# Issuing the later adaLN weight rows from ScalarE's queue instead of the sync engine's

## The chip, the cores and the metric

The kernel runs on one core of one Trainium2 chip, one launch, float32 inputs and output. The metric is the device time of one execution in microseconds (us). The kernel before was timed three times: 1854.41, 1858.54 and 1861.12 us, so the median is 1858.54 us. One execution was profiled; it took 1855.95 us, of which 1854.2 us lie between its first and its last instruction (the span).

## The reference, cut to what matters

One transformer-like layer on 256 tokens of width 2048: a SwiGLU feed-forward (inner width 5632), a token mixer (8 heads of attention with forget gates beside 4 heads of a chunked mLSTM), and a second feed-forward. Each of the three is preceded by a layer norm that is modulated, and followed by a gated residual sum and another layer norm. The modulation comes from one vector `c`, through a matrix of 2048 x 18432 ("ada"):

```python
ada = (jax.nn.silu(c) @ w_ada + b_ada)[:, None, :]
sh1, sc1, g1, sh2, sc2, g2, sh3, sc3, g3 = jnp.split(ada, N_ADA, axis=-1)
h = _swiglu(_modulate(x, sh1, sc1), ffn1_w_in, ffn1_w_out)
x = _layernorm(ALPHA * x + 0.5 * (1 + g1) * h, ln1_g, ln1_b)
h = _token_mixer(_modulate(x, sh2, sc2), w_in, ...)
x = _layernorm(ALPHA * x + (1 + g2) * h, ln2_g, ln2_b)
h = _swiglu(_modulate(x, sh3, sc3), ffn2_w_in, ffn2_w_out)
x = _layernorm(ALPHA * x + 0.5 * (1 + g3) * h, ln3_g, ln3_b)
```

The nine parts of `ada` (three shifts, three scales, three gates) are each 2048 wide. Which of them is needed when is what matters here: `sh1, sc1` before the first feed-forward, `g1` and `sh2, sc2` at its end, `g2` and `sh3, sc3` at the end of the mixer, `g3` at the very end.

## The kernel before, in words

**Weights.** Every weight matrix is streamed through SBUF once, in tiles of 1 MB called `raw` (three buffers, lines 402 to 430). ScalarE rounds half a tile to a `hi` part (the cast at line 155), VectorE subtracts to get the `lo` part (line 156), and TensorE makes three products of each (`hi*hi`, `hi*lo`, `lo*hi`, lines 443 to 447), which keeps float32 accuracy. `hi` and `lo` tiles are 128 x 1024, with six buffers each. A `raw` tile of the first feed-forward gives 24 matmuls of 512 columns: 4 blocks of rows, 2 halves of the tokens, 3 products. A buffer of `raw` is free once both of its `lo` parts are made; a buffer of `hi` is free once TensorE has used it.

**Ada rows.** The matrix `w_ada` is not multiplied on TensorE. It is cut into 18 units of 1024 columns, and each unit into 16 rows of blocks, 128 x 1024 elements or 512 KB. Each such row is loaded into one of two `araw` buffers, and VectorE adds `row * silu(c)` into an accumulator (lines 166 to 171). A unit ends with a split of the accumulator (`ahi`, `alo`, through the same line 155 on ScalarE), a sum over the partitions on TensorE (line 183) and a few VectorE operations. The first four units (the first shift and scale) are loaded at the start by other code. The other 14, 224 rows, are "the later ada rows": they go through `ask` (lines 188 to 192), which takes the next row of the list, gives it an `araw` buffer and issues its load. `ada_rows` (lines 194 to 200) accumulates row k and then asks for row k + 1, whose buffer is that of row k - 1. So the load of a row waits until VectorE has finished the row two before it.

**Pace.** The rows are woven in between the steps over weights: after each 1 MB step, `pump(rate)` lets `rate` rows through on average (line 815: `R_F, R_IN, R_OUT, R_MX, R_A, R_B = 1.25, 1.27, 1.12, 1.26, 1, .7`). `ada.stage` counts the boundaries that were passed: it is 0 during the first feed-forward, set to 1 (line 1198) after the boundary between it and the mixer, and set to 2 (line 1678) after the boundary between the mixer's output projection and the second feed-forward. A boundary is the stretch of residual sum, layer norms and modulation in which TensorE has little to do.

**What sets the order.** Each engine runs its instructions in its own order, and an instruction that has to wait holds up all that stand behind it on that engine. The issue of a DMA is an instruction too, of the engine whose queue it is given to: `SP.dma_start` goes to SyncE, which does nothing else, `S.dma_start` to ScalarE, `G_.dma_start` to GpSimd. A planner orders the instructions of each engine from dependencies and from costs that it assumes, except inside `tc.manual_schedule(...)` blocks, where the written order holds for the named engines (VectorE and ScalarE in the boundaries, lines 685 to 734), and except for `tc.issue_after(...)`, which only puts an instruction behind another on the same engine. The rows are paced with `pinned()` (lines 146 to 151): it ties to instructions of VectorE, so it orders the accumulations and not the loads. Before the change SyncE's queue holds, in one order, the loads of all weights and of the later ada rows. ScalarE issues no DMA at all; beside the casts it does the activations, copies out of PSUM and the copies of transposed tiles.

Of the kernel before, what the change touches and what calls it, by code (L numbers as in the profile page):

```python
# [14 lines left out]
P = 128  # L15
# [17 lines left out]
def layer_kernel(  # L33
# [8 lines left out]
    V, S, G_, PE, SP = nc.vector, nc.scalar, nc.gpsimd, nc.tensor, nc.sync  # L42
# [143 lines left out]
    wanted, asked = [], []  # L186

    def ask():
        if wanted:
            shape, src, tag, k = wanted.pop(0)  # L190
            asked.append(ap.tile(shape, F32, tag="araw", bufs=2, name=f"ar{tag}_{k}"))
            SP.dma_start(asked[-1], src[k * P:(k + 1) * P])

    def ada_rows(acc):
        for k in range(KD):
            if not asked:
                ask()
            ada_acc(acc, asked.pop(0), k)
            ask()
            yield  # L200
# [101 lines left out]
    ada = AdaQueue()  # L302
# [1511 lines left out]
```

## Time and profile before

| | |
|---|---|
| median of the three timed runs | 1858.54 us |
| the profiled execution's own time / its span | 1855.95 us / 1854.2 us |
| TensorE (PE) busy | 1820.5 us, 98% of the span |
| VectorE (DVE) busy | 1452.9 us, 78% |
| ScalarE (ACT) busy | 926.3 us, 50% |
| GpSimd (POOL) busy | 61.7 us, 3% |
| moved by DMA | 510.44 MB, 275 GB/s on average |
| issues of later ada rows on SyncE (line 192) | 224, from 220.6 to 1499.1 us |
| of these before the first boundary / between the two / after the second | 99 / 71 / 54 |

How to read it: busy is the union of an engine's instructions. The records of matmuls overlap, since they are pipelined; a stop of TensorE is seen in the rows that give the idle time before an instruction and what ended it. "SPq" in a row is SyncE's queue; it counts as never busy, and its waits are listed apart. A row "A <- B" in a list of waits means that A stood idle until B had ended; the numbers are the sum in us, how often, and the longest. In rows of the timeline: start, duration (both us), engine, line, operation, what it writes `<-` what it reads, how many were merged, and in brackets the idle time of the engine just before and what ended it.

### The profile page before, as it was taken

The page shows a single profiled execution, that of the slowest core. Times are in us where ns is not written, and L with a number is a line of the kernel's source. Part 1 is how long each engine was busy: PE and PEld are TensorE (multiplying, and loading weights), DVE is VectorE, ACT ScalarE, POOL GpSimd, SP SyncE. Part 2 cuts the span into 40 slices and gives each one's busy share as a digit, 9 for nine tenths or more (in the row PEclk, how much of TensorE's full clock was granted, in tenths as well). Part 3 has the DMA queues.
Part 4 walks back from the last instruction along what each step waited for, and adds up shares of the span by engine and source line. Part 5 has one row for each costly group of instructions (what it writes and reads, how often), then busy time and mean ns, then how long its engine had stood idle before and what let it go on. Part 6 is the DMA issues. An engine that isn't in the chain of part 4 may idle for free.

```text
span 1854.2 us, 25052 instructions
## 1 busy us (share of the span) xinstructions
PE 1820.5 (98%) x9577; PEld 1599.3 (86%) x9577; DVE 1452.9 (78%) x1787; ACT 926.3 (50%) x1332; POOL 61.7 (3%) x92
## 2 busy tenths in 40 slices
PE   7999999999999999999999999999999999999997
PEld 4888888888888888699999887888889999988887
DVE  6889989877787787788889888787997766564655
ACT  3554455443554344755666645555465444554441
POOL 1211100000000000000000000000000000000000
PEclk9999999999999999999999999999999999999999
DMA  9989978988988898489979883998877876666663
GB/s 364 379 293 328 328 231 304 328 308 299 312 294 276 304 305 315 151 295 320 325 264 307 327 298 117 326 347 287 303 255 254 274 233 201 205 204 201 203 202 144
DMA packets 242927, 510.44 MB, mean 275 GB/s; under 512 B 10834, under 2 KB 52466, under 8 KB 241784
## 3 DMA queue, kind: packets, MB, share of 16 engines
q1 hardware_dynamic: 234696, 477.90, 74.7%
q0 software_dynamic: 8112, 30.95, 4.8%
q8 instruction: 75, 1.23, 0.3%
q14 instruction: 44, 0.36, 0.0%
HBM read 506.71 MB, written 2.10 MB: 274 GB/s over the span
## 4 chain that ended last, share of the span: by engine, by line
PE 56%; DVE 1%; issue 1%; ACT 0%; DMA 0%; POOL 0%; DVEq 0%; ACTq 0%; POOLq 0%; SPq 0%
PE gu_f L450 8%; PE o_f L446 4%; PE o_f L445 4%; PE o_f L447 4%; PE gu_f L451 4%; PE fh L446 4%; PE fh L447 4%; PE fh L445 4%; PE o_mx L445 1%; PE o_mx L446 1%; PE o_mx L447 1%; PE b_mv L445 1%; PE b_fv L445 1%; PE pr_m L445 1%; PE b_mv L446 1%; PE b_fv L446 1%
## 5 line engine op out<-in xcount | busy, mean ns | idle before, releaser
L170 DVE SCALAR_TENSOR_TENSOR acc<-ar,csil,acc 128x1024 f32<-128x1024 f32 (+1 forms) x167 | 211.7, 1269 | 65.8 <-DMA ar<-in_w_ada_dram 65.4
L450 PE MATMUL gu_f<-x_f,hi_f2i 128*128 128x512 f32 x640 | 210.0, 382 | 0.0
L451 PE MATMUL gu_f<-x_f,lo_f2i 128*128 128x256 f32 x640 | 174.5, 273 | 0.0
L156 DVE TENSOR_TENSOR lo_f2o<-raw_f2o,hi_f2o 128x1024 fp32r<-128x1024 f32 x86 | 105.2, 1224 | 86.7 <-ACT hi_f2o L155 86.6
L155 ACT CAST hi_s<-raw_s 128x1024 fp32r<-128x1024 f32 x96 | 99.1, 1047 | 117.4 <-PE s L447 64.8
L155 ACT CAST hi_f1o<-raw_f1o 128x1024 fp32r<-128x1024 f32 x86 | 88.4, 1047 | 120.6 <-PE o_f L447 63.3
L155 ACT CAST hi_f2o<-raw_f2o 128x1024 fp32r<-128x1024 f32 x86 | 90.1, 1047 | 115.6 <-PE o_f L447 107.0
L446 PE MATMUL s<-lo_s,x_f 128*128 128x512 f32 x384 | 146.2, 381 | 1.2 <-DVE lo_s L156 1.1
L445 PE MATMUL s<-hi_s,x_f 128*128 128x512 f32 x384 | 146.4, 383 | 0.2 <-ACT x_f L359 0.2
L447 PE MATMUL s<-hi_s,x_f 128*128 128x512 f32 x384 | 145.5, 379 | 0.0
L156 DVE TENSOR_TENSOR lo_f2i<-raw_f2i,hi_f2i 128x1024 fp32r<-128x1024 f32 x80 | 97.9, 1224 | 54.2 <-ACT hi_f2i L155 53.7
L450 PEld LDWEIGHTS gu_f<-x_f,hi_f2i 128*128 128x128 f32 x640 | 121.0, 189 | 16.8
L445 PE MATMUL o_f<-hi_f1o,hi 128*128 128x512 f32 x344 | 131.4, 382 | 3.1 <-DVE hT L1021 2.0
L447 PE MATMUL o_f<-hi_f1o,lo 128*128 128x512 f32 x344 | 131.0, 381 | 0.0
L446 PE MATMUL o_f<-lo_f1o,hi 128*128 128x512 f32 x344 | 131.0, 381 | 0.0
L155 ACT CAST hi_f1i<-raw_f1i 128x1024 fp32r<-128x1024 f32 x80 | 81.1, 1045 | 99.4 <-DMA raw_f1i<-in_ffn_w_in_dram 71.8
L170 DVE SCALAR_TENSOR_TENSOR gate<-ar,csil,gate 128x1024 f32<-128x1024 f32 (+1 forms) x94 | 117.5, 1251 | 16.3 <-DMA ar<-in_w_ada_dram 15.9
L156 DVE TENSOR_TENSOR lo_s<-raw_s,hi_s 128x1024 fp32r<-128x1024 f32 x96 | 115.9, 1220 | 14.8 <-ACT hi_s L155 14.8
L445 PE MATMUL o_f<-hi_f2o,hi 128*128 128x512 f32 x332 | 125.8, 379 | 0.0
L446 PE MATMUL o_f<-lo_f2o,hi 128*128 128x512 f32 x332 | 125.8, 379 | 0.0
L447 PE MATMUL o_f<-hi_f2o,lo 128*128 128x512 f32 x332 | 125.8, 379 | 0.0
L155 ACT CAST hi_fh<-raw_fh 128x1024 fp32r<-128x1024 f32 x80 | 82.4, 1048 | 81.3 <-DMA raw_fh<-in_ffn_w_in_dram 37.0
(447 smaller groups left out, 4830.7 us busy)
## 6 DMA issues: line engine op xcount, KB each, us to landing
ar<-in_w_ada_dram SPq DMA_DIRECT2D x230, 512.0 KB, 5.5
raw_s<-in_ffn_w_in_dram SPq DMA_DIRECT2D x47, 1024.0 KB, 7.6
raw_f1o<-in_ffn_w_out_dram SPq DMA_DIRECT2D x44, 1024.0 KB, 7.3
raw_f2o<-in_ffn_w_out_dram SPq DMA_DIRECT2D x44, 1024.0 KB, 5.0
raw_f1i<-in_ffn_w_in_dram SPq DMA_DIRECT2D x40, 1024.0 KB, 7.5
raw_fh<-in_ffn_w_in_dram SPq DMA_DIRECT2D x40, 1024.0 KB, 7.4
raw_f2i<-in_ffn_w_in_dram SPq DMA_DIRECT2D x40, 1024.0 KB, 5.8
ar<-in_w_ada_dram POOLq DMA_DIRECT2D x45, 512.0 KB, 6.3
```

The costliest lines, as they stand in the source:

```text
L155: S.copy(hi, src)
L156: return V.tensor_tensor(out=lo, in0=src, in1=hi.bitcast(F32), op=ALU.subtract)
L170: V.scalar_tensor_tensor(out=acc, in0=raw, scalar=csil[:, k:k + 1], in1=acc, op0=ALU.mult, op1=ALU.add)
L445: PE.matmul(o, ah, bh, start=start, stop=False)
L446: PE.matmul(o, ah, bl, start=False, stop=False)
L447: PE.matmul(o, al, bh, start=False, stop=stop)
L450: PE.matmul(o, ah, x.rearrange("p s (a n) -> p s n a", a=2), start=start, stop=False)
L451: PE.matmul(o[:, T:], al, woven(x[:, 0]), start=False, stop=stop)
```

## The change

One line: where `ask` issues the load of a row, the queue is chosen by the stage. In stage 1 (the mixer and its output projection) it stays SyncE's; before the first boundary and after the second it is ScalarE's.

```diff
     def ask():
         if wanted:
             shape, src, tag, k = wanted.pop(0)
             asked.append(ap.tile(shape, F32, tag="araw", bufs=2, name=f"ar{tag}_{k}"))
-            SP.dma_start(asked[-1], src[k * P:(k + 1) * P])
+            (SP if ada.stage == 1 else S).dma_start(asked[-1], src[k * P:(k + 1) * P])
```

Nothing else is edited: the rows, their buffers, their pace and the accumulations are the same. The planner orders the whole program anew.

## The prediction

> **What bounds the kernel now.** I read first the page's span and engine rows (busy us, share of the span, instructions), then the busy times by stage.
>
> ```profile
> span 1854.2 us, 25052 instructions
> PE 1820.5 (98%) x9577; PEld 1599.3 (86%) x9577; DVE 1452.9 (78%) x1787; ACT 926.3 (50%) x1332; POOL 61.7 (3%) x92
> ```
>
> The stages are the first feed-forward with its later rows (215 to 750), the first boundary, the mixer (790 to 1128), the second boundary, the second feed-forward with rows, and the rest. After the stretch: TensorE, its weight loads, VectorE, ScalarE, GpSimd busy, then granted clock, DMA share, GB/s.
>
> ```profile
> 215.00:750.00 535.00, 529.83 (x2499) 462.11 (x2498) 431.97 (x450) 242.14 (x302) 6.31 (x10) 1.00 0.86 299
> 750.00:790.00 40.00, 37.39 (x151) 24.43 (x150) 33.37 (x78) 34.78 (x73) 3.06 (x4) 1.00 0.36 123
> ...
> 1160.00:1510.00 350.00, 350.00 (x1809) 311.38 (x1808) 283.03 (x316) 188.91 (x267) 2.20 (x4) 1.00 0.85 290
> 1510.00:1855.00 345.00, 333.78 (x1747) 298.03 (x1746) 208.16 (x235) 147.20 (x174) 4.11 (x4) 0.99 0.58 193
> ```
>
> TensorE sets the end: the change can win only where TensorE stands idle in the two row stretches, and that is 535 - 529.83 = 5.2 us in the first and nothing in the second. TensorE's waits in the first stretch name it all:
>
> ```profile
> PE o_f L445 <- DVE hT L1021: 2.0, 1, 2.0
> PE gu_f L446 <- DVE lo_f1i L156: 1.2, 2, 0.7
> PE o_f L445 <- DVE res L556: 1.1, 1, 1.1
> PE cp L854 <- DVE acc L170: 0.4, 1, 0.4
> PE bc L183 <- DVE alo L156: 0.4, 1, 0.4
> ```
>
> The longest of these cost more than its own length, as the clock granted just after it shows:
>
> ```profile
> 523.55 0.48 PE L445 MATMUL o_f<-hi_f1o,hi 128*128 128x512 f32 x1 [1.97 <-DVE hT L1021]
> ```
> ```profile
> 525.00:530.00 5.00, 5.00 (x17) 4.06 (x16) 4.72 (x5) 3.40 (x6) 0.00 (x0) 0.68 0.65 212
> ```
>
> After 1.97 us of idleness the clock stood at 0.68 for 5 us, 0.32 x 5 = 1.6 us more. So all that can be won is 5.1 + 1.6 = 6.7 us.
>
> **What is moved.** The issues of line 192 on SyncE, first stretch and then second:
>
> ```profile
> L192 SPq DMA_DIRECT2D ar<-in_w_ada_dram x99: 327/367/500, 220.6 to 734.1; - x99
> ...
> DMA to landing us min/median/max: 3.7/5.4/8.8
> ```
> ```profile
> L192 SPq DMA_DIRECT2D ar<-in_w_ada_dram x54: 327/341/368, 1164.3 to 1499.1; - x54
> ```
>
> So 99 + 54 = 153 loads leave SyncE's queue for ScalarE's; 71 stay. With them go their waits. SyncE's, first stretch:
>
> ```profile
> SPq L192 <- DVE acc L170: 122.7, 73, 7.0
> SPq L192 <- DMA ar<-in_w_ada_dram: 78.8, 48, 3.5
> ...
> SPq L192 <- DVE gate L170: 28.5, 15, 5.8
> SPq L192 <- DVE acc L168: 11.7, 6, 4.1
> ...
> SPq L192 <- DVE gate L226: 3.4, 2, 1.7
> ```
> and the two largest of the second:
> ```profile
> SPq L192 <- DVE gate L170: 66.0, 30, 7.7
> ...
> SPq L192 <- DVE acc L170: 50.0, 20, 5.7
> ```
>
> SyncE stands 245.1 us before the first 99 rows, 2.5 us each, and at least 116 us before the other 54, with weights queued behind it.
>
> **Part 1: SyncE is freed; weights are issued earlier.** What a late weight costs stands in ScalarE's casts, first stretch (line, shapes, count | busy us, mean ns | idle before and its causes):
>
> ```profile
> L155 ACT CAST hi_f1o<-raw_f1o 128x1024 fp32r<-128x1024 f32 x86 | 88.4, 1047 | 120.6 <-PE o_f L447 63.3 <-DMA raw_f1o<-in_ffn_w_out_dram 49.7 <-DVE lo_f1o L156 7.6
> L155 ACT CAST hi_f1i<-raw_f1i 128x1024 fp32r<-128x1024 f32 x80 | 81.1, 1045 | 99.4 <-DMA raw_f1i<-in_ffn_w_in_dram 71.8 <-PE gu_f L447 19.4 <-DVE lo_f1i L156 3.4
> L155 ACT CAST hi_s<-raw_s 128x1024 fp32r<-128x1024 f32 x26 | 26.8, 1045 | 24.6 <-PE s L447 13.4 <-DMA raw_s<-in_ffn_w_in_dram 8.8 <-issue 2.3
> ```
>
> The casts waited 71.8 + 49.7 + 8.8 = 130.3 us for weights to land, and 96.1 us for TensorE to free a buffer: the chain runs ahead of TensorE and takes up nearly all of it. A late weight can have caused at most the 1.2 us on `lo_f1i`, and the 2.0 us with its 1.6 of clock: gain 0 to 4.8 us. I take 1.0, near the low end, because weights come as fast as the DMA engines give them: here these are busy 0.86 at 299 GB/s against 0.58 at 193 in the last stretch, so an earlier issue mostly waits there instead. Of the 1.2 us, moreover, this is the larger piece (all engines' timeline):
>
> ```profile
> 458.79 1.28 DVE L170 SCALAR_TENSOR_TENSOR acc<-ar,csil,acc 128x1024 f32<-128x1024 f32 x1 [0.84 <-DMA ar<-in_w_ada_dram]
> ...
> 460.10 0.37 SPq L192 DMA_DIRECT2D ar<-in_w_ada_dram  x1
> ...
> 460.90 1.28 DVE L170 SCALAR_TENSOR_TENSOR acc<-ar,csil,acc 128x1024 f32<-128x1024 f32 x1 [0.83 <-DMA ar<-in_w_ada_dram]
> 461.25 0.38 PE L446 MATMUL gu_f<-lo_f1i,x_f 128*128 128x512 f32 x1
> ...
> 462.11 1.22 DVE L156 TENSOR_TENSOR lo_f1i<-raw_f1i,hi_f1i 128x1024 fp32r<-128x1024 f32 x1
> ...
> 462.22 0.62 ACT L155 CAST ahi<-acc 128x512 fp32r<-128x512 f32 x1 [8.45 <-DVE acc L170]
> 462.33 0.38 PE L445 MATMUL gu_f<-hi_f1i,x_f 128*128 128x512 f32 x1
> ...
> 463.38 0.48 PE L446 MATMUL gu_f<-lo_f1i,x_f 128*128 128x512 f32 x1 [0.67 <-DVE lo_f1i L156]
> ```
>
> VectorE stood 0.84 and 0.83 us for two late **rows**, and the `lo` behind them came 0.67 us late for TensorE. That row is also issued at once: the accumulation ends at 458.79 + 1.28 = 460.07, the issue comes at 460.10. A row cannot go out earlier than now; from ScalarE it can only go later.
>
> **Part 2: ScalarE issues.** No row shows ScalarE issuing a DMA. Bounds: SyncE's 0.33 to 0.50 us above, GpSimd's 0.72 at the median for the same load:
>
> ```profile
> L955 POOL DMA_DIRECT2D ar<-in_w_ada_dram x45: 714/724/889, 43.0 to 217.4; - x45
> ```
>
> I take SyncE's 0.37, the issue of these very loads: 99 x 0.37 = 37 us in the first stretch, where ScalarE is idle 535 - 242.1 = 293 us, and 20 us in the second's 161. Cost 0; even at 0.72 it is 71 of 293. Without that cover it is 0.37 us a row.
>
> **Part 3: rows land later.** A row whose buffer frees while ScalarE is inside a cast waits up to 1.05 us; ScalarE is busy 0.45 of the time, so about 0.24 on average, 24 us over 99 rows, at most 104. VectorE's present waits for rows in the same stretch are the scale:
>
> ```profile
> DVE acc L170 <- DMA ar<-in_w_ada_dram: 42.8, 39, 2.8
> ...
> DVE gate L170 <- DMA ar<-in_w_ada_dram: 8.0, 9, 1.5
> ```
>
> 50.8 us of them cost TensorE the 1.2 us, 0.024 each. So 24 us cost +0.6, 104 us +2.5, and none at all 0.
>
> **Part 4: ScalarE waits.** The wait for the buffer now stands on ScalarE, and behind it the next casts (for `lo` on VectorE, then TensorE), copies and activations. The trace shows one ScalarE instruction that waits for accumulations already, the `ahi` at 462.22, which stood 8.45 us; TensorE's stop there is still explained by VectorE. Bounds: 0, if the planner puts each issue where the buffer is free; 245.1 us, if ScalarE stands as long as SyncE does. ScalarE idles 0.55 of the time anyway, so I count 0.45 of it, 110 us of late casts. At the casts' present rate, (1.2 + 2.0) us of TensorE for 130.3 us waited, 0.025, this is +2.8; bounds 0 and 245 x 0.025 = +6.1. In the second stretch TensorE lost nothing, so I put +0.5, bounds 0 and, with as much again for each row, 54/99 x 6.1 = +3.3.
>
> The page "DMA: Bandwidth & Descriptors" of the Trainium skill (Anatomy of one DMA) speaks against the change: DMA engines do not wait on semaphores, any such wait is on the issuing sequencer before dispatch. By it the 245 us do go to ScalarE; if waits sat in the ring instead, part 4 would be 0 and the sum -0.4. SyncE's rows agree with the page; for ScalarE no row tells.
>
> **Sum:** -1.0 + 0 + 0.6 + 2.8 + 0.5 = +2.9 us on the profiled execution's 1855.95, 1858.9 us. That execution lies 2.6 us below the median of the runs shown, so I forecast 1858.54 + 2.9 = **1861 us**. Its own bounds: -4.8, and +2.5 + 6.1 + 3.3 = +11.9, so 1854 to 1870.
>
> **Rivals.** *Slower: ScalarE is used up in the row bursts.* One matmul takes (462.33 - 461.25) / 5 = 0.216 us, a 1 MB tile's 24 take 5.18, and at 1.27 rows a tile there are 4.08 us per row. ScalarE needs 0.45 x 4.08 = 1.85 of its own, 0.37 to issue and, if it waits as SyncE does, 2.48: 4.70, so 0.62 us is lost per row, 10 us over a unit's 16 rows. The `hi` tiles ahead cover up to five times 12 matmuls, 13 us, when the casts wait for TensorE, and little where they wait for weights; with half, 6.5, each of the six units of the first stretch loses 3.5 us: +21, 1880 us. It decides once ScalarE waits more than 4.08 - 1.85 - 0.37 = 1.86 us per row. For it: SyncE's 2.5, the 8.45. Against: 293 us of idle ScalarE, and a planner that may put issues into it.
>
> *Faster: the freed weight loads end all five waits* and the slow clock: -6.7, 1852 us. For it: 245 us of SyncE standing before weights. Against: 1.1 + 0.4 + 0.4 are VectorE's own order, and the DMA engines are at 0.86.
>
> *No change: the two queues share the DMA engines.* Rows no longer stand behind 1 MB weights and land nearer to 3.7 than 5.4 us, which pays for parts 3 and 4; weights land later by up to the rows' time, 1.27 x 0.52 MB / 299 GB/s = 2.2 us, and are issued up to 2.5 us earlier. The two cancel: 1859 us. The same page (Queues, rings and completion order) has each DMA engine go round-robin between queues by packets, which would do this; with one queue in the trace no row shows it.
>
> **How the numbers follow.** Forecast 0.46, slower rival 0.30, faster 0.12, sharing 0.12. What this kernel's measurement can tell from no change is 0.3%, 5.6 us. Of the forecast's 0.46, 0.09 lies above +5.6 and 0.01 below -5.6. Faster 0.12 + 0.01 = 0.13; same 0.36 + 0.12 = 0.48; slower 0.30 + 0.09 = 0.39. The range reaches to both outer cases, 1852 to 1880.
>
> **What would show it.** Right: line 192 on ScalarE's queue 153 times, issues later than their buffer by up to a cast, more waits of ScalarE's casts behind them, SyncE's weights no longer behind rows, TensorE's idle time in 215 to 750 within a few us of 5.2, the mixer unchanged. For the slower rival: stops of TensorE on `lo` tiles in each unit, with clocks below 1. For the faster: the five rows gone. Wrong would be a time below 1852 or above 1880, or a shift that comes from the boundaries or the mixer, where no row moves.

## The result, and the profile after

The changed kernel takes 1868.64 us (median of 5 runs, 1867.11 to 1875.08) against 1857.45 us for the kernel before (5 runs): ratio 1.0066, 95% interval 1.0043 to 1.0089. It is **slower by 11.2 us**. The profiled execution took 1867.11 us, 11.2 more than that of before, so the two traces differ by as much as the medians.

The page of the changed kernel: its span and the hardware queues (packets, MB, share).

```profile
span 1865.4 us, 25060 instructions
...
q1 hardware_dynamic: 201272, 397.68, 61.8%
q10 hardware_dynamic: 33424, 80.23, 12.6%
```

A second hardware queue, q10, carries the 80 MB of the moved rows (153 of 0.52 MB). The same work by stretches (columns as in the prediction; the kernel now runs about 10 us later from the mixer on):

```profile
215.00:750.00 535.00, 523.57 (x2458) 455.27 (x2457) 428.56 (x444) 242.85 (x302) 5.21 (x9) 0.99 0.85 293
...
800.00:1138.00 338.00, 336.89 (x2338) 316.55 (x2337) 288.41 (x424) 190.88 (x345) 6.61 (x11) 1.00 0.88 303
1170.00:1520.00 350.00, 350.00 (x1807) 311.33 (x1807) 283.55 (x317) 189.91 (x266) 2.20 (x4) 1.00 0.85 290
465.00:470.00 5.00, 5.00 (x17) 4.03 (x17) 5.00 (x6) 3.90 (x6) 0.00 (x0) 0.68 0.86 281
645.00:650.00 5.00, 5.00 (x16) 4.06 (x17) 5.00 (x8) 1.05 (x1) 0.00 (x0) 0.66 0.46 179
```

TensorE is idle 535 - 523.57 = 11.4 us in the first row stretch, where it was 5.2: 6.3 more. Two 5 us slices at clocks of 0.68 and 0.66 cost 1.6 + 1.7 us, where before had one of 1.6: 1.7 more. The mixer lost 1.0 us (before, 790 to 1128: TensorE busy 337.91 of 338). Together 9.0 of the 11.2. The second row stretch lost nothing: 350.00 of 350. Another 1.7 us stands ahead of all the moved rows, where the clock of the changed kernel fell and that of before did not (0.11 of 15 us; before, then after):

```profile
95.00:110.00 15.00, 13.10 (x68) 11.37 (x68) 9.96 (x16) 13.06 (x22) 0.00 (x0) 1.00 0.71 235
95.00:110.00 15.00, 13.27 (x61) 11.32 (x61) 8.78 (x15) 11.64 (x20) 0.00 (x0) 0.89 0.60 199
```

Twelve of the fourteen traces used here have this fall, those of kernels that lose nothing too, so it is not put down to the change.

TensorE's waits in 215 to 750 of the changed kernel (waiting tile, line, what ended it: us, times, longest):

```profile
PE gu_f L446 <- DVE lo_f1i L156: 3.5, 2, 2.1
PE o_f L446 <- DVE lo_f1o L156: 3.4, 2, 1.9
PE o_f L445 <- DVE res L556: 2.1, 1, 2.1
PE o_f L445 <- DVE hT L1021: 1.0, 1, 1.0
PE bc L183 <- DVE alo L156: 0.7, 1, 0.7
PE gu_f L445 <- ACT hi_f1i L155: 0.5, 1, 0.5
PE cp L854 <- DVE acc L170: 0.3, 1, 0.3
```

All but 0.5 us are VectorE's. The moved issues, by line:

```profile
L192 ACTq DMA_DIRECT2D ar<-in_w_ada_dram x153: 334/374/399, 221.2 to 1510.2; - x153
...
DMA to landing us min/median/max: 3.5/5.7/10.2
```

What SyncE waits for now, and then ScalarE, 215 to 750:

```profile
SPq L406 <- DVE lo_f1i L156: 193.1, 38, 10.6
SPq L406 <- DVE lo_f1o L156: 191.1, 40, 8.3
```
```profile
ACT hi_f1o L155 <- DVE acc L170: 38.8, 20, 4.0
ACT hi_f1i L155 <- DVE acc L170: 33.6, 14, 5.1
...
ACT hi_f1i L155 <- DMA raw_f1i<-in_ffn_w_in_dram: 18.7, 9, 4.4
...
ACT hi_f1i L155 <- DVE gate L170: 12.4, 7, 3.2
ACT hi_f1o L155 <- DMA raw_f1o<-in_ffn_w_out_dram: 9.8, 7, 3.8
```

The waits changed places as the code says. SyncE waits almost only for the weights' own buffers. ScalarE's casts stand behind accumulations (110 us over all its waits for rows' accumulations; before 19.3, all of `ahi`), and their waits for weights to land fell from 130.3 us to 35.3 (18.7 + 9.8 + 6.8 for `raw_s`). Yet TensorE's stops grew, and nearly all of them wait for VectorE, whose own waits the prediction read only for rows. Before, and then after:

```profile
DVE acc L170 <- DMA ar<-in_w_ada_dram: 42.8, 39, 2.8
DVE lo_f1i L156 <- ACT hi_f1i L155: 18.5, 10, 4.0
DVE lo_f1o L156 <- ACT hi_f1o L155: 16.1, 10, 3.9
DVE gate L170 <- DMA ar<-in_w_ada_dram: 8.0, 9, 1.5
DVE o_f L554 <- PE o_f L447: 6.2, 1, 6.2
DVE hT L1063 <- PE s L447: 3.5, 2, 1.9
...
DVE lo_s L156 <- ACT hi_s L155: 1.6, 3, 0.7
```
```profile
DVE acc L170 <- DMA ar<-in_w_ada_dram: 53.8, 33, 3.8
DVE lo_f1i L156 <- ACT hi_f1i L155: 16.2, 13, 3.5
DVE lo_f1o L156 <- ACT hi_f1o L155: 12.1, 11, 4.6
DVE gate L170 <- DMA ar<-in_w_ada_dram: 9.2, 6, 2.6
...
DVE lo_s L156 <- ACT hi_s L155: 4.0, 6, 1.6
DVE hT L1063 <- PE s L447: 1.9, 1, 1.9
```

Before: 50.8 us for rows and 36.2 for `hi` casts, 87.0 together. With its 432.0 us of work that is 519 of 535; it waited only 11.2 us for TensorE (`o_f`, `hT` and 1.5 of small ones), so that it had little in hand: 11.2 us at most, since a wait in one place does not make good a late `lo` in another. After: 63.0 + 32.3 = 95.3, 8.3 us more; the waits for TensorE fell to 3.4, and TensorE lost 6.3 us of idleness and 1.7 of clock. The longest stop shows how, on VectorE, ScalarE with its queue, and TensorE (start, length, instruction, in brackets the wait):

```profile
459.16 1.28 DVE L170 SCALAR_TENSOR_TENSOR acc<-ar,csil,acc 128x1024 f32<-128x1024 f32 x1 [0.55 <-DMA ar<-in_w_ada_dram]
462.18 1.28 DVE L170 SCALAR_TENSOR_TENSOR acc<-ar,csil,acc 128x1024 f32<-128x1024 f32 x1 [1.73 <-DMA ar<-in_w_ada_dram]
463.38 2.35 DVE L156 TENSOR_TENSOR lo_f1i<-raw_f1i,hi_f1i 128x1024 fp32r<-128x1024 f32 x2
```
```profile
457.51 3.35 ACTq L192 DMA_DIRECT2D ar<-in_w_ada_dram  x2
460.97 1.99 ACT L155 CAST hi_f1i<-raw_f1i 128x1024 fp32r<-128x1024 f32 x2 [3.19 <-DVE acc L170]
```
```profile
462.07 0.48 PE L445 MATMUL gu_f<-hi_f1i,x_f 128*128 128x512 f32 x1 [0.51 <-ACT hi_f1i L155]
464.66 0.70 PE L446 MATMUL gu_f<-lo_f1i,x_f 128*128 128x512 f32 x1 [2.10 <-DVE lo_f1i L156]
```

Both suspects stand in it: the cast came 3.19 us late behind the issue of two rows, and the `lo` that it feeds stood behind an accumulation that waited 1.73 us for its row.

### The profile page after: what moved, and what is told of

It is laid out like the page before. It is cut to its first block, busy times and chain, and to the rows that moved or that the text cites. A ratio compares the mean times of both kernels' runs of the same rounds, so it can differ in the third digit from the quotient of the medians.

```text
span 1865.4 us, 25060 instructions
## 1 busy us (share of the span) xinstructions
PE 1825.2 (98%) x9577; PEld 1602.1 (86%) x9577; DVE 1452.6 (78%) x1787; ACT 927.3 (50%) x1332; POOL 61.6 (3%) x92
## 3 DMA queue, kind: packets, MB, share of 16 engines
q10 hardware_dynamic: 33424, 80.23, 12.6%
## 4 chain that ended last, share of the span: by engine, by line
PE 53%; DVE 3%; DMA 1%; issue 1%; ACT 1%; POOL 0%; DVEq 0%; ACTq 0%; POOLq 0%
PE gu_f L450 8%; PE o_f L446 4%; PE o_f L445 4%; PE o_f L447 4%; PE gu_f L451 4%; PE fh L445 4%; PE fh L446 4%; PE fh L447 4%; PE o_mx L447 1%; PE o_mx L445 1%; PE o_mx L446 1%; DMA ar<-in_w_ada_dram 1%; PE b_mv L445 1%; PE pr_m L445 1%; PE b_mv L446 1%
## 5 line engine op out<-in xcount | busy, mean ns | idle before, releaser
L155 ACT CAST hi_f1o<-raw_f1o 128x1024 fp32r<-128x1024 f32 x86 | 88.3, 1046 | 114.1 <-PE o_f L447 44.8
L170 DVE SCALAR_TENSOR_TENSOR gate<-ar,csil,gate 128x1024 f32<-128x1024 f32 (+1 forms) x94 | 117.6, 1252 | 21.2 <-DMA ar<-in_w_ada_dram 21.1
L446 PE MATMUL gu_f<-lo_f1i,x_f 128*128 128x512 f32 x320 | 122.2, 382 | 3.5 <-DVE lo_f1i L156 3.5
```

What stands on the lines that cost most here:

```text
L155: S.copy(hi, src)
L170: V.scalar_tensor_tensor(out=acc, in0=raw, scalar=csil[:, k:k + 1], in1=acc, op0=ALU.mult, op1=ALU.add)
L446: PE.matmul(o, ah, bl, start=False, stop=False)
```

## The experiments

Three theories. **W**: ScalarE stands in the rows' waits, its casts come late. **O**: the planner, which orders VectorE's instructions, has moved them: comparing the two programs, 34 of 288 accumulations stand one or two `lo` splits earlier than before and 1 later, so they wait for rows ahead of `lo` splits that could run. (TensorE's order is the same in both programs; of ScalarE's instructions some 40 stand elsewhere, and no run held those.) **R**: with two queues the rows come later to VectorE, whatever ScalarE does; either because the queues share the DMA engines (R1) or because SyncE, freed, issues its weights earlier (R2).

Each run below was timed in 5 rounds beside the kernel before on the same chip. One table for all; the last three columns are of 215 to 750, the waits summed from VectorE's (for rows, and of `lo` splits for `hi` casts).

| kernel | rows' queue | VectorE's order | ratio to before [95%] | VectorE waits, rows + `hi` | VectorE waits for TensorE | TensorE idle |
|---|---|---|---|---|---|---|
| before | SyncE | before's | 1 | 50.8 + 36.2 = 87.0 | 11.2 | 5.2 |
| after | ScalarE | after's | 1.0066 [1.0043, 1.0089] | 63.0 + 32.3 = 95.3 | 3.4 | 11.4 |
| act_old_order | ScalarE | before's | 1.0076 [1.0052, 1.0099] | 52.7 + 42.7 = 95.4 | 3.4 | 12.8 |
| sp_new_order | SyncE | after's | 1.0054 [1.0035, 1.0072] | 64.8 + 33.0 = 97.8 | 3.8 | 11.2 |
| sp_issue_act_waits | SyncE | late | 1.0003 [0.9990, 1.0017] | 44.0 + 35.0 = 79.0 | 12.3 | 4.5 |
| sp_late_order | SyncE | late | 1.0009 [0.9990, 1.0028] | 45.2 + 36.7 = 81.9 | 12.0 | 4.1 |
| pool_issue | GpSimd | its own | 1.0067 [1.0043, 1.0090] | 68.1 + 24.2 = 92.3 | 3.1 | 9.5 |
| pool_old_order | GpSimd | before's | 1.0075 [1.0052, 1.0098] | 71.3 + 21.2 = 92.5 | 5.7 | 11.9 |
| pool_late_order | GpSimd | late | 1.0065 [1.0045, 1.0086] | 65.3 + 23.0 = 88.3 | 5.3 | 8.7 |
| act_late_order | ScalarE | late | 1.0079 [1.0052, 1.0106] | 56.7 + 35.9 = 92.6 | 4.3 | 11.0 |
| act_old_held | ScalarE | before's | 1.0077 [1.0051, 1.0103] | 53.1 + 44.7 = 97.8 | 4.8 | 15.0 |
| sp_three_buffers | SyncE | its own | 1.0057 [1.0035, 1.0079] | 15.8 + 26.5 = 42.3 | 50.2 | 0.5 |
| act_three_buffers | ScalarE | its own | 1.0061 [1.0040, 1.0082] | 24.3 + 24.4 = 48.7 | 45.4 | 0.1 |
| act_three_sixth | ScalarE | its own | 0.9963 [0.9949, 0.9978] | 21.7 + 21.5 = 43.2 | 45.6 | 0.5 |

**Order against queue.** VectorE's 1767 instructions are held to a written order, by edges that set the order of issue and no wait. The kernel before, held to its own order, is the same sequence on every engine, so holding adds nothing.

```diff
+    info = mybir.DependencyInfo(mybir.DependencyClass.NoSync, mybir.DependencyReason.DATA)
+    for order in ORDERS:
+        at = [nc.find_inst_by_name("I-" + n) for n in order.split()]
+        for one, two in zip(at, at[1:]):
+            tc.add_manual_dep(two, one.name, info, reason="written order")
```

> The later rows are issued from ScalarE as in the change, but VectorE's instructions are held to the order that they had before it (353 of them stand elsewhere in the changed kernel, the accumulations of line 170 earlier relative to the `lo` splits of line 156). Theory W (ScalarE stands in waits for accumulations, its casts come late, TensorE stops on `lo`): the order of VectorE has no part in it, the time stays 8 to 14 us above before. Theory O (VectorE's new order puts accumulations that wait for rows ahead of the `lo` splits): the loss goes, within 3 us of before, TensorE's idle time in 215 to 750 back from 11.4 to about 5 us. Theory R (rows land later, or two queues share the DMA engines): it stays, 8 to 14 us above.

Measured 1872.57 against 1857.37 us: the loss stays, with the old order. O alone does not carry it. By the table VectorE waits 8.4 us more than in before, 1.9 of them for rows and 6.5 for `hi` casts; the second is the mark of W.

> The counterpart: the later rows are issued from SyncE as before, and VectorE's instructions are held to the order of the changed kernel. Theory W: no wait on ScalarE, so within 3 us of before. Theory O: 8 to 12 us above before, with TensorE's stops of 2 to 3 us on `lo` tiles in 215 to 750. Theory R: the rows go out and land as before, within 3 us of before. If both crossings lie halfway, order and queue each carry a part.

Measured 1868.12 us, 10.7 above before, with one queue and no wait on ScalarE (SyncE's loads were replanned a little beside it). So the new order **alone** costs as much as the change, and the queue with the old order costs as much too; together they cost no more than either. The prices do not add, which suggests that they meet in one place.

**ScalarE's wait alone.** Rows on SyncE; ScalarE writes one column of the row's buffer first, so that the row goes out 0.29 us after its buffer is free (median, worked out row by row) instead of 0.03.

```diff
+            if ada.stage != 1:
+                t = asked[-1]
+                S.copy(t[:, :1] if len(shape) == 2 else t[:, 0, :1], mhalf[:, :1])
             SP.dma_start(asked[-1], src[k * P:(k + 1) * P])
```

> The rows stay on SyncE, but before each of the 153 later loads ScalarE writes one column of the same buffer, which the load then overwrites: ScalarE waits for the buffer exactly as in the change, without a DMA issue or a second queue. Theory W: most of the loss, 6 to 12 us above before. Theory R by two queues: none of it, within 3 us; R by late rows: some of it, since the load now waits for ScalarE also. Theory O: it goes by what the planner does with the order; if VectorE's order stays as before, within 3 us.

Measured 1858.77 us: no loss. Its ScalarE waits, 215 to 750 (three lines lower for the added ones):

```profile
ACT ar L194 <- DVE acc L170: 108.6, 57, 5.4
...
ACT ar L194 <- DVE gate L170: 19.2, 11, 3.3
```

127.8 us of ScalarE standing for accumulations before the rows' loads alone, more than the 110 in all of the changed kernel, and TensorE idle 4.5 us. In this order of VectorE, W by itself costs nothing. But the order is not before's: the planner put 10 accumulations one `lo` split **later** here. W alone in before's order was not run; the next runs carry the late order to the other queues.

**Another queue without ScalarE's waits.** One word changes: the later rows go to GpSimd's queue.

```diff
-            SP.dma_start(asked[-1], src[k * P:(k + 1) * P])
+            (SP if ada.stage == 1 else G_).dma_start(asked[-1], src[k * P:(k + 1) * P])
```

> The 153 later loads are issued from GpSimd's queue, so that SyncE is free of them as in the change, two queues share the DMA engines, and ScalarE waits for nothing. Theory W: within 3 us of before or a little below it. Theory R by two queues: 8 to 12 us above. Theory O: as the planner orders VectorE; with the accumulations early again, above before.

> The later rows from GpSimd's queue, VectorE's instructions held to the order of the kernel before (in the run from GpSimd's queue above, 33 of 288 accumulations stood one or two `lo` splits earlier). Theory O (VectorE's order): within 3 us of before. Theory R (two queues share the DMA engines, rows land later): 8 to 14 us above, as with ScalarE's queue in the old order. Theory W (the waits on ScalarE) has no part here: within 3 us of before. So O and W together stand or fall against R.

Measured 1871.13 us in the planner's order and 1871.31 us in before's, both some 13.8 above before. The stretch and VectorE's waits of the second:

```profile
215.00:750.00 535.00, 523.10 (x2451) 455.21 (x2450) 430.04 (x444) 241.85 (x302) 70.23 (x107) 0.99 0.84 294
```
```profile
DVE acc L170 <- DMA ar<-in_w_ada_dram: 53.6, 36, 3.8
DVE gate L170 <- DMA ar<-in_w_ada_dram: 17.7, 9, 4.0
```

Rows alone: 71.3 us waited for them against 50.8, with `hi` waits down to 21.2. So rows that come later are enough for the loss, where W and O are out. That the sharing of the DMA engines makes them late is not shown by it: GpSimd's issue takes 722 ns and comes 0.30 us after the buffer is free (worked out row by row; SyncE and ScalarE 0.03), and 0.30 us on each of 99 rows is 30 us, more than the 20.5 that were added.

**The late order on each queue.**

> The later rows from ScalarE as in the change, VectorE's instructions held to the order of the run in which ScalarE waited and SyncE issued (10 of 288 accumulations stand one or two `lo` splits later than before; that run lost nothing). Theory O: within 3 us of before. Theory W: the buffers come free later still, so ScalarE stands longer: 12 to 18 us above. Theory R: 8 to 14 us above.

> The later rows from GpSimd's queue with the same later order of VectorE. Theory O: within 3 us of before, or some us below it, since SyncE's 1 MB loads no longer stand behind rows and the `lo` splits come first. Theory R: 8 to 14 us above. Theory W: as before, within 3 us.

> Control: the rows from SyncE as before, with only the later order of VectorE. All theories: within 3 us of before, since VectorE's `lo` splits are if anything earlier; if it is 3 us or more below, the later order alone is a gain, which the runs with it have to be measured against.

Measured 1871.79, 1868.22 and 1859.24 us, against 1857.52 for before on that chip. With one order of VectorE, SyncE loses nothing (with ScalarE's wait or without), GpSimd 10.7 and ScalarE 14.3 us. From a row's issue to the accumulation that stood waiting for it, averaged in 215 to 750, took 5.51 us on SyncE, 5.70 on GpSimd (issued 0.3 later besides) and 6.10 on ScalarE; in before's order 5.58, 5.79 and 6.00. In the changed kernel's own order it was 5.68 on SyncE and 5.67 on ScalarE, and 5.41 from GpSimd in the order that the planner gave it. Each of these is a mean of 39 to 48 rows of one trace that scatter by 1.2 to 1.4 us, so it is uncertain by about 0.2; and the median from issue to landing, 5.3 us on SyncE in the late order and 5.4 in before's, was 5.3 and 5.2 on GpSimd and 5.3 and 5.9 on ScalarE. So the runs show what each queue costs in the late order, and not that a second queue makes each row slower. ScalarE's waits without its queue cost nothing there, so its 14.3 us need the queue; a part for W beside R is not excluded.

**Is it the freed SyncE?** ScalarE's queue, before's order, and weights that wait again as they did behind rows:

```diff
+    wait = mybir.DependencyInfo(mybir.DependencyClass.Sync, mybir.DependencyReason.DATA)
+    for pair in HELD.split():
+        load, row_free = [nc.find_inst_by_name("I-" + n) for n in pair.split(":")]
+        tc.add_manual_dep(load, row_free.name, wait, reason="as behind the row")
```

> As the run from ScalarE in the old order of VectorE (1872.6 us, +15), but SyncE's weight loads wait again for what they waited for before: each of the 107 loads that stood right behind a later row in SyncE's queue now waits for the same accumulation that this row waits for. What is told apart is why rows take longer with two queues (in 215 to 750, from issue to the accumulation that waited for it, 5.58 us before, 6.00 in that run, 5.8 from GpSimd's queue). Theory R1 (two queues share the DMA engines, whatever SyncE does): stays 10 to 16 us above before. Theory R2 (SyncE, freed of the rows' waits, issues its 1 MB weights as soon as their buffers are free, and they compete with the rows): within 5 us of before, rows back to about 5.6 us. Theory W (ScalarE stands in waits): stays 10 to 16 us above, with rows at about 5.6.

Measured 1875.71 us, 17.6 above: nothing came back (rows 5.81 us). SyncE stood again before its weights:

```profile
SPq L406 <- DVE acc L170: 82.5, 13, 9.5
```

R2 is not the cause by itself. There was also little to hold: in before, the loads of `raw_f1i` and `raw_f1o` went out 0.03 us after their buffer was free at the median and 0.55 in the mean (worked out load by load). What makes the second queue dear stays open: the sharing itself (R1), ScalarE's waits and replanned casts in its runs, GpSimd's later issue in its own. No run takes one of these away while it keeps the second queue.

**Three row buffers.** If all of it acts through the round trip of a row in two buffers (buffer free, load issued and landed, row accumulated, buffer free again), a third must make queue and order indifferent. SBUF has room for it only without one `lo` tile.

```diff
-    wp.tile([P, 1024], F32R, tag="lo", bufs=6, name="lo_place")
+    wp.tile([P, 1024], F32R, tag="lo", bufs=5, name="lo_place")
...
-            asked.append(ap.tile(shape, F32, tag="araw", bufs=2, name=f"ar{tag}_{k}"))
+            asked.append(ap.tile(shape, F32, tag="araw", bufs=3, name=f"ar{tag}_{k}"))
```

> Control for the next: the kernel before with three buffers for the rows instead of two, and five `lo` tiles instead of six to make room. If the round trip of a row through two buffers is what holds VectorE in the bursts, its waits for rows (50.8 us in 215 to 750) fall to under 15 us and the five stops of TensorE mostly go: 3 to 7 us below before. If the sixth `lo` tile matters more, slower by some us.

> The change with three buffers for the rows and five `lo` tiles. Theory R (either kind): a row may land 0.4 us later without VectorE waiting for it, so the loss goes: within 3 us of the control. Theory O: with the rows there, an accumulation that stands early waits for nothing, so within 3 us of the control as well. Theory W: each wait of ScalarE for a buffer is shorter, but the waits stay; some of the loss stays, 3 to 8 us above the control.

Measured 1870.75 and 1870.76 us: the queue makes no difference any more, as R and O expected. W is not excluded by it, since with the third buffer ScalarE's waits for accumulations fell too, from 110 to 46 us. But both are 12.6 us above before, where I expected SyncE's 3 to 7 below. By stretch, SyncE's:

```profile
215.00:750.00 535.00, 534.55 (x2535) 468.10 (x2534) 434.13 (x452) 246.73 (x305) 3.88 (x8) 1.00 0.86 301
750.00:790.00 40.00, 33.34 (x124) 20.39 (x123) 33.69 (x77) 33.27 (x72) 3.76 (x4) 0.91 0.36 119
```

The row stretch is what it should be: 0.5 us of TensorE idle, and 0.1 with ScalarE's queue, instead of 5.2 and 11.4. VectorE's waits for rows are 15.8 and 24.3 us. The loss stands at the boundaries: 33.34 of 40 us at a clock of 0.91, where before had 37.39 at 1.00, and as much at the second (1128 to 1175: 41.23 of 47 at 0.93, before 45.92 at 1.00). Their cause is the tile that was taken. SyncE's run, VectorE's timeline and TensorE's wait:

```profile
744.23 1.23 DVE L156 TENSOR_TENSOR lo_f1o<-raw_f1o,hi_f1o 128x1024 fp32r<-128x1024 f32 x1 [10.57 <-PE o_f L447]
```
```profile
PE tp L378 <- DVE n L372: 5.6, 1, 5.6
```

The end of an output projection holds six `lo` tiles until its last products; with five, VectorE waits for one and begins the boundary late.

**Both.** So the sixth `lo` there, and the boundary's own sixth, are put into a row buffer; no row needs it at that time.

```diff
+    def lo_tile(shape, name, sixth):
+        if sixth:
+            return ap.tile(shape, F32R, tag="araw", bufs=3, name=name)
+        return wp.tile(shape, F32R, tag="lo", bufs=5, name=name)
...
-            lo = wp.tile([P, h, w], F32R, tag="lo", bufs=6, name=f"lo_{name}{q}")
+            lo = lo_tile([P, h, w], f"lo_{name}{q}", sixth and q == nk // h - 1)
...
-                                         f"{tag}o{col}_{u}", into=into):
+                                         f"{tag}o{col}_{u}", into=into, sixth=lastg and i == nu - 1):
...
-            ws.append((k, hi, wp.tile([P, 1024], F32R, tag="lo", bufs=6, name=f"lo_{tag}e{k}")))
+            ws.append((k, hi, lo_tile([P, 1024], f"lo_{tag}e{k}", k == 5)))
```

> The change with three row buffers and five `lo` tiles, where the sixth `lo` that the end of each output projection and the boundaries hold lies in a row buffer. The run with three buffers had TensorE's stops in 215 to 750 down to 1.8 us, but stood 5.8 us at each boundary, where VectorE waited 10.6 us for TensorE to give back a `lo` tile. Theory R: the rows' round trip was the whole price of the change; with the boundaries' stop back at 0.8 us each, this is 10 us under that run (1870.8) and below the kernel before by 2 to 8 us. If the boundary's stop comes from VectorE's own chain there and not from the `lo` tile, it stays near 1870. If theory W or O had a part that three buffers do not cure, 3 us or more of stops on `lo` tiles would stand in the row stretch.

Measured 1852.22 against 1859.66 us, ratio 0.9963 (0.9949 to 0.9978): **7.4 us faster than the kernel before**, with the rows on ScalarE's queue. The stretch, and all that TensorE waits for in 215 to 790:

```profile
215.00:750.00 535.00, 534.46 (x2534) 467.95 (x2532) 439.01 (x470) 251.01 (x312) 4.94 (x7) 1.00 0.84 299
```
```profile
PE tp L378 <- ACT n L374: 2.0, 3, 1.0
PE tp L378 <- DVE n L372: 0.6, 1, 0.6
```

No stop of TensorE is left in the row stretch, with the change in place. It is 18.5 us under the run with three buffers alone, where the expectation had 10: that counted the boundaries' stops, and left out the slow clock behind them (0.09 of 40 us and 0.07 of 47, 6.9 us in all). The same buffers on SyncE's queue were not run, so the gain is that of the third buffer and not shown to be the queue's.

## Why the prediction was right and wrong

The time fell inside the range, above the likeliest value; "slower" had 0.39, "same" 0.48. The range was wide, 1852 to 1880, and the terms of the sum give 2.9 of the 11.2 us, by a price that did not hold, so that the hit is luck as far as the mechanism goes. By its steps:

- **What bounds the kernel**: right that TensorE sets the end and that the second stretch has nothing to lose or win (350.00 of 350). It missed that VectorE, with 432 us of work and 87 of waits for rows and casts in 535, waited only 11.2 us for TensorE and so had little in hand. Those rows stood in the trace of before.
- **Part 1, earlier weights, -1.0**: the casts' waits for weights fell by 95 us, but hardly because weights came earlier. They fell as far, to 39.8 us, in the run where the rows stayed on SyncE and ScalarE waited, and not at all from GpSimd's queue (126.6 in before's order): the casts came later. Nothing was won: the stop on `lo_f1i` that this was to take went from 1.2 to 3.5 us. The reason given, that this stop was two late rows, was right.
- **Part 2, 0.37 us per issue at no cost**: 374 ns each, in ScalarE's idle time (busy 242.85 of 535): the length is right; that it cost nothing is not separated by a run.
- **Part 3, later rows, +0.6**: wrong in its mechanism. ScalarE already stands at the issue when the buffer frees; the row goes out 0.03 us after, no cast in between. VectorE's waits for rows still rose by 12.2 us, half of the 24 assumed; the new order of accumulations, which the step did not think of, gives as much with SyncE's queue (64.8 us in all, against 63.0).
- **Part 4, 110 us of ScalarE's waits, +2.8**: ScalarE waits 91 us more for accumulations than before, against 110 assumed. The page "DMA: Bandwidth & Descriptors" of the Trainium skill (Anatomy of one DMA) puts such waits on the issuing sequencer, and the trace agrees, with these 91 us. But the `lo` splits did not wait longer for their casts (32.3 us against 36.2; with before's order held they did, 42.7), and as much waiting without the second queue cost nothing in the late order.
- **The step that failed is the price per us in parts 3 and 4**, 0.024 and 0.025 of TensorE's time for each us waited. It divides one small stop, the same 1.2 us in both parts, by waits that had cost TensorE nothing because VectorE could still catch up. Here 8.3 us more of VectorE's waits went with 6.3 us of TensorE's idleness and 1.7 of clock, about one for one. That is no fixed price either: from 87.0 us (before) to 88.3 (pool_late_order) TensorE's idle time rises by 3.5 us. In the table each kernel with two buffers and 87 us or less loses nothing against before, and each with 88 to 98 loses 10 to 18 us; with three buffers the sum is under 49 and in the row stretch neither order nor queue counts. At the measured 8.3 us and one for one, the sum would have been -1.0 + 8.3 = +7.3, nearer the measured 11.2. The sum also has no term for the new order of VectorE, which alone cost 10.7 us (sp_new_order).
- **The rivals**: "slower" had the wrong place (ScalarE used up in each of six units; the stops are few, on VectorE's `lo` and `res`). "No change" had rows land nearer to 3.7 us than 5.4 and weights later: the median from issue to landing in 215 to 750 was 5.0 us for the rows, and 7.1 and 7.6 for the weights `raw_f1o` and `raw_f1i` against 7.3 and 7.5 before, so the exchange that it counted on is not there. The same page of the Trainium skill (Queues, rings and completion order) has the engines alternate between queues; the trace shows q1 and q10 side by side, but no run shows the alternation itself.
- **The mixer unchanged**: nearly; it lost 1.0 us, though no row moved there.

## What to carry to other kernels

Price a delay by what is left in hand on the engine that it delays, its waits for the engine that sets the end, and not by the average of what past waits cost: here that engine waited 11 us in 535, and 8 us more of delay cost about as much. When a transfer cycles through two buffers, its round trip is part of the consumer's time; here another queue and another order each cost about the same, alone or together, and with a third buffer TensorE no longer stopped in the row stretch. Moving an issue also moves the planner's order on engines that the change never names, so compare the orders before explaining a wait.

## What the runs showed of the hardware

- A load issued from ScalarE takes 374 ns of its sequencer, as from SyncE (367); from GpSimd 722. On ScalarE and SyncE the issue follows the buffer's release by 0.03 us at the median, on GpSimd by 0.30.
- Putting 512 KB rows on a queue of their own did not bring them clearly sooner. In 215 to 750, the median from issue to landing was 5.4 us on the weights' queue, 5.2 from GpSimd's and 5.9 from ScalarE's with VectorE in before's order, 5.3 on all three in the late order, and 5.3 on the weights' queue and 5.0 from ScalarE's in the changed kernel's order.
- Stops of TensorE of 2.10 us (before the matmul at 464.66) and 2.08 us (for `res`) were each followed by 5 us at a clock of 0.66 to 0.68, as the 1.97 us of before was, so that such a stop cost nearly twice its length. A stop of 1.93 us (718.35, for `lo_f1o`) was not:

```profile
715.00:725.00 10.00, 8.07 (x38) 6.75 (x37) 9.93 (x12) 5.21 (x6) 0.00 (x0) 1.00 0.77 258
```
